# Three embedding blocks computed ahead of the first projection, and three filler units fewer in the attention of a one-core hybrid encoder step

## The chip, the cores and the metric

The kernel runs on one core of a Trainium2 chip. The metric is the device time of one execution in microseconds. The profile is one execution, taken by the hardware profiler; its times are counted from the start of its span. The engines are PE (TensorE: matrix products; PEld is its loading of weights), DVE (VectorE), ACT (ScalarE), POOL (GpSimd) and SP, which here only issues DMAs.

## The reference

One layer of a streaming encoder, on 1056 frames (1024 of a prompt and 32 of a sample) of width 1024:

- RMSNorm, then one projection whose columns are queries, keys and values of 8 heads, three parts of a gated convolution, and two sets of sigmoid gates ("gates", 2 x 1024 columns);
- stick-breaking attention (no softmax: products of 1 - beta over the keys between), and a causal convolution of width 3;
- both branches projected, weighed by their gates, summed, projected, added to x;
- RMSNorm, an MLP with squared ReLU (4096 wide), added to x;
- `x = x + sigmoid(rmsnorm(x) @ w_ple_gate) * (p @ w_ple)`, where p (1056 x 256) is an input of its own; then a final RMSNorm.

The change is about `p @ w_ple`. It depends on inputs alone, and the kernel calls its eight column blocks of 128 the embeddings. They are needed only in the last stage.

## The kernel before, in words

Everything is kept transposed: 128 features on the partitions, frames along the free axis. A float32 product is made of three products of rounded parts: each operand is split into a high part (ACT casts it, `fp32r`) and a low part (DVE subtracts the high part), and high x high, high x low and low x high are summed in PSUM.

The stages are: the first gates (lines 590 to 628), the rest of the input projection by a seven-product scheme (`seven`, line 209), the attention (lines 1062 to 1091), the branches and the output projection, the MLP (`up` and `down`), and the last stage with the embeddings. Inside a stage that stands under `tc.manual_schedule` the order on PE, ACT, DVE and POOL is the order in which the code issues the work. SP's order, and the branches, are placed by the framework's scheduler.

**The start.** SP issues, in this order, the weights of the first gate block, the first quarter of x in four pieces (`load_x`, line 285), the weights of the second block, and the other x. `vecT` goes through ACT's queue. In `first_gates` a round makes one group of 24 products, 264 columns wide. `prepare_plain` (line 162) casts and splits a block of weights (lines 98 and 99), `parts_x` (line 323) makes the high (line 329) and low (`mix`, line 142) parts of x, for eight pieces in the order 0, 2, 4, 6, 1, 3, 5, 7. The group's products are lines 203, 204 and 205; line 597 copies a finished group from PSUM. A pool `wraw` holds four blocks of raw weights, `wsp` two of split ones, `bpool` 34 buffers of one row block each. Six PSUM buffers take the groups in turn (`group`).

**The attention.** It has 64 steps: 4 pairs of heads, 2 heads each, 8 blocks of queries (step index i from 0 to 7, with i + 1 key blocks). The steps are software-pipelined by hand. In each round of the loop, in the order "LSAFBFG": L runs DVE's scan of the step before (line 799), S the scores of this step (PE lines 781 and 782, ACT sigmoid line 785, POOL mask line 792), A and B turn the weights of two steps before (PE line 835, ACT line 838, DVE line 839), G multiplies with the values (PE line 854) and F fills.

**Filler units.** F gives PE work that is free of the attention: gate blocks 10 to 15 (four units each, a unit being 24 products of 264 columns) and the eight embeddings (`embed_unit`, one unit each: 3 column tiles of 352, six products each, lines 735 to 737, an ACT copy of each tile, line 738, and one write to DRAM). They go in that order. Six units run before the attention (`START`), the other 26 (`FILL`) in it. `last_gates`, which holds gate blocks 14 and 15, also loads p and `w_ple` (`p_fetch`) and, after one of its groups each, splits the two halves of p (`p_parts`) and the two halves of `w_ple` (`embed_weights`). These four splits therefore come after 15, 16, 17 and 18 units of the attention's fill.

`pace` (line 1033) shares the units over the steps. It works out a load for every step from the sizes of three neighbouring steps, by and large DVE's work, and PE's own work; a step's part of FILL is what PE's own work leaves open of a fixed multiple of its load. Four times it adds 1.25 of load where the fill passes `FILL - 11 + more`:

```python
for more in (0, 1, 2, 3, None):
    unit = (FILL * 2.92 + sum(own)) / sum(load)
    part = [max(0.0, unit * v - o) for v, o in zip(load, own)]
    part = [x * FILL / sum(part) for x in part]
    ends = [sum(part[: n + 1]) for n in range(ns + 2)]
    if more is not None:
        load[next(n for n, e in enumerate(ends) if e > FILL - 11 + more)] += 1.25
```

## Time and profile before

| | us |
|---|---|
| median of 3 runs | 1553.07 |
| lowest and highest run | 1552.27, 1553.09 |
| the profiled execution's own time | 1552.95 |
| its span, first to last instruction | 1551.3 |
| PE, DVE, ACT busy | 1523.2, 1065.5, 745.2 |

The span is what the profile shows; the time holds 1.65 us more around it. A line of the profile names the engine, the line of the kernel, the operation, and what it writes and reads (`out<-in`, buffer numbers left out) with partitions x elements. "Idle before" is the engine's idle time just before the instruction, and the arrow names what ended it. PE's products overlap: each lasts longer than the time from its start to that of the next, so the pace is read from the start times. The first product starts at 6.17 us; the attention's scans run from 394.4 to 578.9.

### The profile page before, as it was taken

What the parts mean: (1) busy time and instruction counts of PE and PEld (TensorE: products, weight loads), DVE (VectorE), ACT (ScalarE), POOL (GpSimd) and SP (SyncE); (2) the same over time, 40 slices, a digit from 0 to 9 for tenths busy, and PEclk for the clock granted to TensorE, in tenths of its full rate; (3) what the DMA queues carried; (4) which work ended last, traced back from release to release, by engine and by line L of the source; (5) the groups of instructions that cost most, each with busy time, mean ns of one, the idle gap of its engine ahead of it and who ended that gap; (6) DMA issues with size and microseconds to landing.
All of it is one profiled execution on the core that took longest, in us unless ns stands there. A gap on an engine that the chain in (4) does not pass through costs nothing.

```text
span 1551.3 us, 29314 instructions
## 1 busy us (share of the span) xinstructions
PE 1523.2 (98%) x11770; PEld 1507.9 (97%) x11770; DVE 1065.5 (69%) x1414; ACT 745.2 (48%) x1357; POOL 347.3 (22%) x296
## 2 busy tenths in 40 slices
PE   8999999999999999999999999999999999999996
PEld 7999999999899999999999999999999999999996
DVE  7544776666778886766667555554577987799766
ACT  6643344443566774333355555555533334434544
POOL 1222332220211114001312222221020222013353
PEclk9999999999999999999999999999999999999998
DMA  6532155544635566335454344434886897583433
GB/s 230 199 113 78 34 184 201 191 151 115 210 100 153 167 222 231 98 129 180 162 187 147 138 142 149 153 132 144 295 305 201 264 343 250 191 269 109 134 116 118
DMA packets 111159, 268.97 MB, mean 173 GB/s; under 512 B 13456, under 2 KB 29328, under 8 KB 111024
## 3 DMA queue, kind: packets, MB, share of 16 engines
q1 hardware_dynamic: 110880, 267.08, 51.0%
q8 instruction: 92, 1.51, 0.4%
q14 instruction: 43, 0.35, 0.1%
q10 hardware_dynamic: 144, 0.03, 0.0%
HBM read 186.33 MB, written 80.73 MB: 172 GB/s over the span
## 4 chain that ended last, share of the span: by engine, by line
PE 86%; DVE 6%; ACT 2%; issue 2%; POOL 2%; DMA 2%; SPq 0%; DVEq 0%; POOLq 0%; ACTq 0%
PE ps_dn L1449 7%; PE ps_dn L1448 7%; PE ps_dn L1450 7%; PE ps_A11u L204 4%; PE ps_A11u L205 4%; PE ps_A11u L203 4%; PE ps_A11i L205 3%; PE ps_A11i L203 3%; PE ps_A11i L204 3%; PE av L854 2%; PE ps_wo L107 2%; PE ps_wo L108 2%; PE ps_wo L109 2%; PE ps_S1u L204 2%; PE ps_S1u L205 2%
## 5 line engine op out<-in xcount | busy, mean ns | idle before, releaser
L1449 PE MATMUL ps_dn<-fl,whi_dn 128*128 128x264 f32 x896 | 254.8, 284 | 0.1
L1450 PE MATMUL ps_dn<-fh,wlo_dn 128*128 128x264 f32 x896 | 254.8, 284 | 0.0
L1448 PE MATMUL ps_dn<-fh,whi_dn 128*128 128x264 f32 x896 | 254.8, 284 | 0.0
L1449 PEld LDWEIGHTS ps_dn<-fl,whi_dn 128*128 128x128 f32 x896 | 168.6, 188 | 0.4 <-DVE fl L1357 0.4
L1450 PEld LDWEIGHTS ps_dn<-fh,wlo_dn 128*128 128x128 f32 x896 | 168.7, 188 | 0.0
L1448 PEld LDWEIGHTS ps_dn<-fh,whi_dn 128*128 128x128 f32 x896 | 168.6, 188 | 0.0
L190 POOL TENSOR_TENSOR s_i<-raw_i,raw_i 128x512 f32<-128x512 f32 x30 | 40.8, 1359 | 228.9 <-DVE slS_i L153 196.0
L1341 DVE TENSOR_TENSOR wlo_dn<-raw_dn,whi_dn 128x1024 fp32r<-128x1024 f32 x40 | 71.0, 1776 | 25.5 <-ACT whi_dn L1335 24.9
L799 DVE TENSOR_TENSOR_SCAN r<-r 128x128 f32<-128x128 f32 (+3 forms) x64 | 86.6, 1353 | 2.2 <-POOL r L792 2.1
L1335 ACT CAST whi_dn<-raw_dn 128x1024 fp32r<-128x1024 f32 x40 | 42.0, 1051 | 93.3 <-PE ps_dn L1449 79.1
L190 POOL TENSOR_TENSOR s_u<-raw_u,raw_u 128x512 f32<-128x512 f32 x30 | 44.6, 1488 | 186.7 <-DVE slS_u L153 157.8
L1390 POOL TENSOR_TENSOR c<-c,rs 128x528 f32<-128x528 f32 x16 | 26.8, 1673 | 244.4 <-DVE c L1457 122.7
L1357 DVE TENSOR_TENSOR fl<-mr,fh 128x1056 fp32r<-128x1056 f32 x56 | 69.7, 1246 | 4.4 <-ACT fh L1352 4.4
L792 POOL TENSOR_SCALAR_AFFINE_SELECT r<-r 128x128 f32<-128x128 f32 x64 | 26.0, 407 | 204.5 <-ACT r L785 204.4
L153 DVE TENSOR_TENSOR slS_i<-s_i,shS_i 128x512 fp32r<-128x512 f32 x45 | 35.3, 788 | 51.7 <-ACT shS_i L151 51.5
L203 PE MATMUL ps_A11u<-T,shS_u 128*128 128x264 f32 x240 | 68.5, 285 | 0.0
L203 PE MATMUL ps_A11i<-T,shS_i 128*128 128x264 f32 x240 | 68.5, 285 | 0.0
L205 PE MATMUL ps_A11i<-T,slS_i 128*128 128x264 f32 x240 | 68.4, 285 | 0.0
L204 PE MATMUL ps_A11u<-T,shS_u 128*128 128x264 f32 x240 | 68.2, 284 | 0.0
L204 PE MATMUL ps_A11i<-T,shS_i 128*128 128x264 f32 x240 | 68.2, 284 | 0.0
L205 PE MATMUL ps_A11u<-T,slS_u 128*128 128x264 f32 x240 | 68.2, 284 | 0.0
L839 DVE TENSOR_TENSOR at<-pa,at 128x512 fp32r<-128x512 f32 (+2 forms) x96 | 50.9, 550 | 19.7 <-ACT at L838 19.3
(428 smaller groups left out, 5594.5 us busy)
## 6 DMA issues: line engine op xcount, KB each, us to landing
raw_dn<-in_w_down_dram SPq DMA_DIRECT2D x56, 512.0 KB, 4.5
raw_i<-in_w_in_dram SPq DMA_DIRECT2D x34, 512.0 KB, 4.6
mr<-mdT SPq DMA_DIRECT2D x32, 528.0 KB, 5.3
raw_u<-in_w_up_dram SPq DMA_DIRECT2D x32, 512.0 KB, 3.5
mdB<-m SPq DMA_DIRECT2D x48, 264.0 KB, 2.4
mr<-mdB SPq DMA_DIRECT2D x24, 528.0 KB, 6.3
raw_pg<-in_w_ple_gate_dram SPq DMA_DIRECT2D x17, 512.0 KB, 3.5
s<-gd SPq DMA_DIRECT2D x16, 528.0 KB, 5.6
```

What stands on the lines that cost most here:

```text
L190: f()
L203: nc.tensor.matmul(p_, wh[:, k, :], o[:, 0, c], start=new and n == 0, stop=False, **on)
L204: nc.tensor.matmul(p_, wh[:, k, :], o[:, 1, c], start=False, stop=False, **on)
L205: nc.tensor.matmul(p_, wl[:, k, :], o[:, 0, c], start=False, stop=z, **on)
L799: nc.vector.tensor_tensor_scan(rev, rev, rev, 1.0, ALU.mult, ALU.bypass)
L839: nc.vector.tensor_tensor(al, pt[:, :nb, :], ah.bitcast(F32), op=ALU.subtract)
L1335: nc.scalar.copy(hi, dws[u])
L1341: dve(lo, raw, hi.bitcast(F32), op=sub)
L1357: dve(l, mraw.pop(v), opd[v].bitcast(F32), op=sub)
L1448: nc.tensor.matmul(ps, hi[:, j, :], oh, start=j == 0, stop=False)
L1449: nc.tensor.matmul(ps, hi[:, j, :], ol, start=False, stop=False)
L1450: nc.tensor.matmul(ps, lo[:, j, :], oh, start=False, stop=j == NP_ - 1)
```

## The change

Ahead of all other loads SP now fetches the first three blocks of `w_ple` and p, p in three column tiles of each half. `first_embeds`, called before the first gates, multiplies a tile of ones with itself seven times (`WARM`), splits weights and p, and computes embeddings 0, 1 and 2 for all three column tiles: 9 groups of 6 products. Of the nine copies from PSUM the first three stand at its end on ACT, the middle three on DVE between the two halves of the first `parts_x`, the last three on ACT ahead of the second `parts_x`. The filler keeps embeddings 3 to 7, so `FILL` is 23. The later load of `w_ple` takes the five blocks that are left, two in the first half and three in the second; p is loaded a second time as before.

```diff
-FILL = 26.0
+FILL = 23.0
+FIRST_EMBEDS = 3
+WARM = 7
...
+    NE = FIRST_EMBEDS
+    pw_first = wraw.tile([P, NE, 2, P], F32, tag="raw", name="raw_pw_first")
+    nc.sync.dma_start(pw_first, w_ple[:, :NE])
+    p_first = [blk(f"pf{f}") for f in range(2)]
+    for c in ts:
+        for f in range(2):
+            nc.sync.dma_start(p_first[f][:, c], pT[f][:, c])
     n_ = base["g"]
     raws["i0"] = [raw_w(w_in, n_, KD, "i0_0")]
...
+    def first_embeds():
+
+        wu = gps.tile([P, TW], F32, tag="g", name="warm")
+        for _ in range(WARM):
+            nc.tensor.matmul(wu[:, :P], ones, ones, start=True, stop=True)
+        wh = wsp.tile([P, NE, 2, P], F32R, tag="whi", name="whi_pw_first")
+        wl = wsp.tile([P, NE, 2, P], F32R, tag="wlo", name="wlo_pw_first")
+        h, l = ([blk(f"pf{x}{f}", F32R) for f in range(2)] for x in "hl")
+        e = [blk(f"em{n}") for n in range(NE)]
+        late = []
+
+        def out():
+            n, c, ps = late.pop(0)
+            (nc.vector.tensor_copy if c is ts[1] else nc.scalar.copy)(e[n][:, c], ps)
+            if c is ts[-1]:
+                nc.sync.dma_start(ed[n], e[n])
+
+        nc.scalar.copy(wh, pw_first)
+        for i, c in enumerate(ts):
+            for f in range(2):
+                r = p_first[f][:, c]
+                nc.scalar.copy(h[f][:, c], r)
+                if i + f == 0:
+                    dve(wl, pw_first, wh.bitcast(F32), op=sub)
+                dve(l[f][:, c], r, h[f][:, c].bitcast(F32), op=sub)
+            for n in range(NE):
+                ps = group(f"ps_pw{n}_{i}")
+                for k in range(2):
+                    nc.tensor.matmul(ps, wh[:, n, k, :], h[k][:, c], start=k == 0, stop=False)
+                for k in range(2):
+                    nc.tensor.matmul(ps, wl[:, n, k, :], h[k][:, c], start=False, stop=False)
+                for k in range(2):
+                    nc.tensor.matmul(ps, wh[:, n, k, :], l[k][:, c], start=False, stop=k == 1)
+                late.append((n, c, ps))
+        for _ in range(NE):
+            out()
+        return out
...
-                parts_x(0, near_)
+                parts_x(0, near_, (0, 2, 4, 6))
+                for _ in range(NE):
+                    embed_out()
+                parts_x(0, near_, (1, 3, 5, 7))
                 prepare_plain("i0", 1)
             elif n in (1, 3):
+                if n == 1:
+                    for _ in range(NE):
+                        embed_out()
                 parts_x(n // 2, far_ if n == 1 else whole_)
...
-            pwr.append(wraw.tile([P, 4, 2, P], F32, tag="raw", name=f"raw_pw{i}"))
-            nc.sync.dma_start(pwr[i], w_ple[:, 4 * i : 4 * i + 4])
+            pwr.append(wraw.tile([P, 3, 2, P], F32, tag="raw", name=f"raw_pw{i}"))
+            nc.sync.dma_start(pwr[i][:, 1 - i :], w_ple[:, 3 + 2 * i : 5 + 3 * i])
...
-    units += [embed_unit(n) for n in range(KD)]
+    units += [embed_unit(n) for n in range(NE, KD)]
...
         nc.scalar.preload_act_table_set("sqrt_and_others")
+        embed_out = first_embeds()
         run(first_gates())
```

More of the change, by code (lines that the diff above doesn't have):

```diff
@@ L718, in embed_weights @@
     def embed_weights(i):
-        h, l = (blk(f"pw{i}{x}", F32R, [P, 4, 2, P]) for x in "hl")
-        nc.scalar.copy(h, pwr[i])
-        dve(l, pwr[i], h.bitcast(F32), op=sub)
+        h, l = (blk(f"pw{i}{x}", F32R, [P, 3, 2, P])[:, 1 - i :] for x in "hl")
+        nc.scalar.copy(h, pwr[i][:, 1 - i :])
+        dve(l, pwr[i][:, 1 - i :], h.bitcast(F32), op=sub)
         pw.append((h, l))
@@ L729, in body @@
                 conv_parts(n - 3)
-            wh, wl = (x[:, n % 4] for x in pw[n // 4])
+            wh, wl = (x[:, n - (3 if n < 5 else 5)] for x in pw[n >= 5])
             e = blk(f"em{n}")
```

## The prediction

> **What bounds the kernel now.** I read the page first: its busy rows and the chain of waits by engine.

> ```profile
> span 1551.3 us, 29314 instructions
> PE 1523.2 (98%) x11770; PEld 1507.9 (97%) x11770; DVE 1065.5 (69%) x1414; ACT 745.2 (48%) x1357; POOL 347.3 (22%) x296
> PE 86%; DVE 6%; ACT 2%; issue 2%; POOL 2%; DMA 2%; SPq 0%; DVEq 0%; POOLq 0%; ACTq 0%
> ```

> TensorE is busy 98% of the span and carries 86% of the chain. The change takes no product away: it moves 54 from the attention to the start and adds seven idle ones. So it can win only where PE now stands still or runs slowly, and can lose only where another engine gets too little PE work beside it. Two stretches decide: the first 13 us and the attention (about 394 to 586). First the timeline of the start (start, duration, engine, line):

> ```profile
> 0.80 0.39 SPq L89 DMA_DIRECT2D raw_i<-in_w_in_dram  x1
> 0.90 0.17 DVE L76 MEMSET ones<- 128x128 f32 x1 [0.90 <-PEq L1823]
> 1.25 1.96 SPq L287 DMA_DIRECT2D x<-in_xf_dram  x4
> 4.66 1.04 ACT L98 CAST whi_i<-raw_i 128x1024 fp32r<-128x1024 f32 x1 [2.14 <-DMA raw_i<-in_w_in_dram]
> 6.17 0.59 PE L203 MATMUL ps_g<-B,whi_i 128*128 128x264 f32 x1 [6.17 <-ACT B L329]
> 7.71 2.14 ACT L329 ACTIVATE B<-x,vecT 128x264 fp32r<-128x264 f32 x5 [0.22 <-DMA x<-in_xf_dram]
> 8.02 0.42 PE L203 MATMUL ps_g<-B,whi_i 128*128 128x264 f32 x1
> 10.00 0.42 PE L203 MATMUL ps_g<-B,whi_i 128*128 128x264 f32 x1
> 10.53 0.30 PE L203 MATMUL ps_g<-B,whi_i 128*128 128x264 f32 x1
> 11.76 0.28 PE L204 MATMUL ps_g<-B,whi_i 128*128 128x264 f32 x1
> 12.09 0.39 PE L205 MATMUL ps_g<-B,wlo_i 128*128 128x264 f32 x1
> ```

> PE does nothing for 6.17 us. From 8.02 to 10.00 nine products start 0.22 us apart; from 10.53 to 11.76 ten start 0.123 apart. So the first 4 us of work run at about half pace. The product at 12.09 is the 27th (third of the second gate group) and the last that waits early. At full pace 26 products take 3.2 us, so the gate stream stands as if it had begun at 8.9.

> The windows view shows the full clock even there, so half pace is read from start times, not from that column (PE, PEld, DVE, ACT, POOL, clock, DMA share, GB/s):

> ```profile
> 0.00:10.00 10.00, 3.17 (x12) 2.87 (x13) 4.36 (x11) 6.07 (x11) 0.70 (x6) 1.00 0.82 281
> 10.00:15.00 5.00, 4.95 (x39) 4.73 (x39) 4.56 (x10) 4.41 (x10) 0.00 (x0) 1.00 1.06 389
> 448.50:469.10 20.60, 20.60 (x165) 20.06 (x164) 19.13 (x27) 14.34 (x34) 3.17 (x8) 1.00 0.44 133
> 469.10:489.00 19.90, 19.90 (x159) 19.34 (x158) 18.07 (x26) 12.89 (x31) 2.90 (x8) 1.00 0.58 164
> 514.50:537.50 23.00, 22.70 (x161) 21.26 (x160) 21.00 (x29) 17.26 (x40) 5.10 (x8) 1.00 0.62 194
> ```

> The last three are rounds of eight attention steps. PE is full, but DVE works 19.13 of 20.60 us: PE bounds, with DVE 7 to 9% behind. Who makes PE wait in the attention (total, times, longest):

> ```profile
> PE z L781 <- ACT r L785: 1.0, 2, 0.5
> PE pa L835 <- DVE r L799: 1.0, 2, 0.8
> ```

> **The change part by part.** *Taken from the attention.* Two products five apart within one embedding group, and the group's ACT copy:

> ```profile
> 581.23 0.33 PE L736 MATMUL ps_pw<-p0l,pw1h 128*128 128x352 f32 x1
> 582.04 0.60 PE L835 MATMUL pa<-ident,r 128*128 128x128 f32 x4
> L738 ACT COPY em<-ps_pw 128x352 f32<-128x352 f32 x24 | 11.0, 457 | 4.9 <-PE ps_pw L737 4.5
> ```

> Five products in 0.81 us, 0.1625 each. Three units are 54 products: 54 x 0.1625 = **8.8 us** less PE work, and nine copies (4.1 us) less on ACT.

> *The start.* Seven DMAs (384 KB of weights, six of 176 KB; 1.47 MB) go ahead of everything in SP's queue. At 389 GB/s everything behind them lands 3.8 us later. I time the path from the rows above and these, of the groups of the first 40 us:

> ```profile
> L146 ACT CAST T<-x 128x528 fp32r<-128x528 f32 x7 | 4.1, 632 | 0.0
> L147 DVE TENSOR_TENSOR T<-x,T 128x528 fp32r<-128x528 f32 x7 | 4.5, 691 | 0.0
> L99 DVE TENSOR_TENSOR wlo_i<-raw_i,whi_i 128x1024 fp32r<-128x1024 f32 x4 | 4.9, 1217 | 5.1 <-ACT whi_i L98 5.1
> L597 ACT COPY sg<-ps_g 128x264 f32<-128x264 f32 x9 | 3.4, 374 | 3.7 <-PE ps_g L205 3.6
> ```

> The first weights land at 4.66 less 128 KB (0.34 us): 4.3; the pieces of p follow 0.46 apart, 4.8 to 7.1. ACT: high part of the weights (three quarters of 1.04) to 5.1, then six pieces. No 352-wide cast from SBUF is in the trace; it lies between 0.374 (264 wide) and 0.632 (528); I take 0.40, nearest the first: done at 5.5, 5.9, ... 7.5. DVE: low weights (three quarters of 1.217) to 6.0, then low pieces, bounded by half and whole of 0.691; I take 0.5: 6.5, 7.0, ... 9.0. The first group's sixth product needs the second low piece: it ends at about 7.15. Nothing is late for the other 48: 48 x 0.1625 = 7.8, so the embeddings end at **14.95** at full pace.

> Is the gate work ready then? Gate weights land at 4.66 + 3.8 = 8.5; ACT is first done with the three early copies (9.55), casts to 10.6, and makes eight high parts at 0.43 (2.14 / 5) by 14.05. Their last x lands at 7.7 + 3.8 = 11.5, read at 11.9. DVE follows to 11.8, four low parts to 13.5, three copies to 14.9, four low parts to 16.5. The first of those is needed by the 14th gate product, 14.95 + 13 x 0.123 = 16.55, and is ready at 15.3. The second gate weights wait for the buffer that the last embedding product frees: cast to 16.0, low part behind DVE's queue to 17.75, needed at 18.15. So no wait, if only by 0.4 us. The later x are used one, two gate groups on, with the same distance as now. The three writes of finished embeddings stand in SP's queue between the weights of the next set and wait for the last copies (17.4); behind them waits

> ```profile
> POOL s_i L190 <- DMA raw_i<-in_w_in_dram: 22.5, 1, 22.5
> ```

> POOL, whose sums before began at 22.6 and are first multiplied after 16 gate groups (8.9 + 16 x 2.95 = 56): 30 us of room, so no cost.

> The 27th gate product then starts at 14.95 + 3.2 = 18.15 instead of 12.09: **+6.1 us**, for 8.8 us of work done.

> *The clock.* The ones are set at 1.07, so seven products run from about 1.1. What they last, from the same kind (ones against a full-float tile: nine products in 18 instructions, first and last start given):

> ```profile
> L391 PE MATMUL pr<-dg,ones x18: 195/275/377, 83.6 to 85.6; 128*128 128x128 f32 x16, 128*128 128x32 f32 x2
> ```

> 2.0 us over 17 steps is 0.118 per instruction; seven products are 14, at half pace 0.21 each: 3.0 us, until 4.1. Then 1.4 us idle until 5.5. Before, about 4 us of work ended half pace. Price of no effect: from 7.15 to 9.6 products at 0.29 instead of 0.1625, some 6.6 lost: 1.1 us. I count full pace.

> [...]

> *What the attention gives back.* Its planner shares FILL over the steps by DVE load. Working through pace(): a round gets 2.25 to 2.34 units instead of 2.68, 1.0 to 1.2 us less PE work. DVE's free time there is 1.5 (20.60 - 19.13) and 1.8 us: covered. Two places are not.

> First, entry. To 406.98 the chain is not PE's:

> ```profile
> 397.44 3.98 DMA q<-qd
> 405.37 1.56 DVE r L799
> 406.98 0.66 PE pa L835 x4
> ```

> Units left out of steps 0 to 4 (1.99 to 1.82, 0.5 us) only lengthen that wait.

> Second, the planner adds 1.25 of load at four fill positions from FILL - 11 on, where p and its weights are split. Those splits hang in gate units, which stay at positions 15 to 18; the four bumps now stand at 12 to 15. Before, bumps fell on steps 37, 39, 40, 44 and splits on 39, 40, 40, 44. Now bumps fall on 32, 35, 38, 40 and splits on about 40, 43, 47, 49.

> ```profile
> L115 DVE TENSOR_TENSOR p0l<-pr,p0h 128x1056 fp32r<-128x1056 f32 x1 | 1.3, 1259 | 0.2 <-ACT p0h L114 0.2
> L721 DVE TENSOR_TENSOR pw0l<-raw_pw,pw0h 128x1024 fp32r<-128x1024 f32 x1 | 1.2, 1225 | 0.3 <-ACT pw0h L720 0.3
> L99 DVE TENSOR_TENSOR wlo_oc<-raw_oc,whi_oc 128x512 fp32r<-128x512 f32 x2 | 1.4, 684 | 0.0
> ```

> Each bump is 0.44 unit, 1.3 us of PE work; three are misplaced: 3.9 us without cover. DVE's free time over those ten steps, 1.9 us, takes up half. I count 2.0 us of new PE waits (bounds: minus the 1.0 us that PE now waits for ACT, if fewer copies end that; plus 3.9).

> **Sum:** +6.1 - 8.8 + 0.5 + 2.0 = -0.2 us on the profiled execution's 1552.95. The median of the runs is 1553.07, 0.1 higher; I predict 1552.8.

> **Rivals.** (a) *The attention pays in full*: DVE's slack hides the misplaced bumps and the ACT waits go: +6.1 - 9.8, and -0.6 if loads and splits come a little earlier: -4, 1549. For it: PE waits little on DVE before, with rounds at 91 to 93%. Against: round 514.5 has DVE at 21.00 of 23.00 and already 0.3 us of PE gap, with its bumps in place. (b) *The attention becomes DVE's*: around steps 40 to 50 every uncovered microsecond turns into a PE wait (3.9 and the entry 0.5, plus 1 where ACT's p casts hold up a sigmoid): +6.1 - 8.8 + 5.4 = +2.7, with the cold clock +3.8: 1556.7. It turns slower once the new waits exceed 2.7 us. (c) *The ones do not hold the clock*: +1.1, 1553.9 with the rest as forecast; that part then doesn't do what it says.

> **Numbers.** A measurement of this kernel tells about 0.2%, 3.1 us, from no change. Forecast, with (c) on its own inside the same band: 0.64. (a) beyond -3.1: 0.20. (b) beyond +3.1: 0.16. The range reaches into (a) and (b): 1549.4 to 1556.2.

> **What would show it.** Third product of the second gate group at 18.1; earlier is better. Embedding products at 0.16 from the first (0.29: (c)). Attention from first to last scan shorter by about 6 us; new "PE pa <- DVE r" waits of about 2 us near steps 43 to 50, their absence means (a), over 4 us (b). Behind the attention nothing should move. The forecast is wrong if gate weights, not PE, end the start, or if the early loads of the next weights hold up POOL's sums.

## The result, and the profile after

| | before | changed | ratio, 95% interval |
|---|---|---|---|
| first comparison, median (lowest to highest, runs) | 1552.89 (1552.27 to 1553.84, 6) | 1558.79 (1556.17 to 1560.41, 6) | 1.0034 [1.0022, 1.0045] |
| on another chip (e1) | 1553.04 (1551.55 to 1556.34, 19) | 1556.95 (1555.47 to 1557.99, 11) | 1.0021 [1.0012, 1.0030] |
| profiled execution, span | 1551.3 | 1558.1 | |

The change makes the kernel slower, by 3.9 to 5.9 us. The forecast was 1552.8 with a range up to 1556.2. The changed kernel's page, answering to the three lines shown first of before:

```profile
span 1558.1 us, 29376 instructions
PE 1527.9 (98%) x11784; PEld 1510.7 (97%) x11784; DVE 1073.9 (69%) x1424; ACT 746.2 (48%) x1361; POOL 353.8 (23%) x296
PE 86%; DVE 5%; issue 3%; ACT 2%; POOL 2%; DMA 1%; SPq 0%; POOLq 0%; DVEq 0%; ACTq 0%
```

The page alone says nothing: 4.7 us more PE time, and nearly the same shares. The places are told by comparing start times of the same instructions (us later than before; first run: the profiled execution above; e1: the same kernel again; e9: a variant below):

| | before at | changed | e1 | e9 |
|---|---|---|---|---|
| 27th gate product | 12.09 | +8.3 | +9.1 | +9.2 |
| first seven-product group | 56.64 | +9.2 | +8.8 | +8.8 |
| first scan of the attention | 394.40 | +8.4 | +7.5 | +7.8 |
| first conv-branch product | 582.60 | +4.2 | +3.2 | +3.5 |
| first attention-branch product | 631.81 | +8.0 | +5.1 | +3.5 |
| end of span | 1551.30 | +6.8 | +4.0 | +2.3 |

So the start costs 8 to 9 us, the attention gives 4.3 back, and the branch stage behind it, in which nothing was to move, takes 2 to 4 us in two of the three. The start of the changed kernel (timeline; a row may join equal instructions, "x2"):

```profile
0.80 0.39 SPq L296 DMA_DIRECT2D raw_pw_first<-in_w_ple_dram  x1
5.27 0.33 SPq L91 DMA_DIRECT2D raw_i<-in_w_in_dram  x1
5.11 0.83 ACT L349 CAST whi_pw_first<-raw_pw_first 128x768 fp32r<-128x768 f32 x1 [2.58 <-DMA raw_pw_first<-in_w_ple_dram]
5.84 2.56 ACT L353 CAST pfh<-pf 128x352 fp32r<-128x352 f32 x6
12.07 1.05 ACT L100 CAST whi_i<-raw_i 128x1024 fp32r<-128x1024 f32 x1
1.12 3.33 PE L336 MATMUL warm<-ones 128*128 128x128 f32 x14 [1.12 <-DVE eps_t L80]
6.38 0.82 PE L360 MATMUL ps_pw<-pfh,whi_pw_first 128*128 128x352 f32 x2 [1.93 <-ACT pfh L353]
8.90 0.79 PE L362 MATMUL ps_pw<-pfh,wlo_pw_first 128*128 128x352 f32 x2
17.27 0.28 PE L205 MATMUL ps_g<-B,whi_i 128*128 128x264 f32 x1
20.41 0.28 PE L207 MATMUL ps_g<-B,wlo_i 128*128 128x264 f32 x1
```

The first weights are cast at 5.11 instead of 4.3, the first embedding product runs at 6.38 instead of 5.5 (PE's first useful product before ran at 6.17: the embeddings start no earlier than the gates did), from 8.31 to 10.66 pairs of products stand 0.59 apart (0.29 each), and the gates begin at 17.27. There was no wait between the embeddings and the gates, as forecast, and the 27th product follows 3.14 later (3.2 forecast). In this one profile the clock column tells more (windows, columns as in the prediction):

```profile
4.30:7.71 3.41, 1.49 (x6) 0.86 (x5) 1.74 (x3) 2.60 (x6) 0.00 (x0) 1.00 1.01 354
7.71:11.12 3.41, 3.40 (x12) 3.27 (x12) 1.83 (x5) 1.60 (x4) 0.00 (x0) 0.50 0.97 319
```

The column's first entry in this trace is at 4.30, at the end of the ones (1.12 to 4.45), and it is 1.00; PE was busy for only 1.49 of the 3.41 us from there, and the next 3.41 us ran at 0.50.

Rounds of eight scans in the attention (windows, columns as before; 1st and 2nd answer to the first two rounds shown of before, the 3rd to the third), and the branch stage:

```profile
454.85:475.49 20.64, 20.36 (x159) 19.28 (x158) 19.11 (x27) 14.12 (x32) 4.54 (x8) 1.00 0.53 141
475.49:497.13 21.64, 20.61 (x161) 19.47 (x160) 19.16 (x26) 13.80 (x32) 4.42 (x8) 1.00 0.52 159
521.82:544.57 22.75, 21.87 (x170) 20.54 (x169) 20.45 (x29) 16.29 (x39) 4.63 (x8) 1.00 0.40 124
```
```profile
610.00:614.00 4.00, 3.45 (x20) 2.87 (x18) 3.45 (x2) 2.58 (x3) 3.72 (x2) 1.00 0.94 373
614.00:618.00 4.00, 2.75 (x9) 2.76 (x10) 4.00 (x3) 1.08 (x1) 3.35 (x2) 0.66 0.24 74
```
```profile
614.00:618.00 4.00, 4.00 (x26) 3.95 (x26) 3.20 (x6) 2.35 (x3) 0.00 (x0) 1.00 0.63 235
```

The last fence is the kernel before. The first round did not get shorter (20.60 before); it is a weak witness, because it holds nearly the same filler work (60 filler products against 61), but PE now has gaps, of 0.3 to 1.0 us in each of the three. In the branch stage PE has 9 products in 4 us where before had 26, with the clock column at 0.66. What PE waited for in the attention (engine, line, total us, times, longest):

```profile
PE pa L888 <- DVE r L852: 2.2, 4, 0.8
PE z L834 <- ACT r L838: 1.7, 4, 0.5
PE pas L1069 <- DMA raw_pw<-in_w_ple_dram: 1.5, 1, 1.5
```

Before, the first two were 1.0 and 1.0, and the third was not there. Its row names a DMA that `pas` does not read; in e1 the same wait is put down to DVE's `oT` (line 812), and in the timeline of this profile `oT` ends at 424.60, behind a scan of 2.02 us, and the product starts at 424.65. It too is a wait for DVE. The branch stage's timeline shows what PE waits for:

```profile
611.51 3.13 POOL L941 TENSOR_TENSOR s<-s,rs 128x1056 f32<-128x1056 f32 x1 [0.28 <-DMA raw_oc<-in_w_conv_out_dram]
612.89 2.30 DVE L101 TENSOR_TENSOR wlo_oc<-raw_oc,whi_oc 128x512 fp32r<-128x512 f32 x1 [0.55 <-ACT whi_oc L100]
615.25 0.66 PE L111 MATMUL ps_oc<-cv,wlo_oc 128*128 128x352 f32 x1 [1.75 <-DVE wlo_oc L101]
615.70 0.49 PE L109 MATMUL ps_oc<-cv,whi_oc 128*128 128x352 f32 x1
```

DVE's low part of the weights takes 2.30 us beside a POOL multiplication (0.68 to 0.69 in the three of this stage that have none beside them); PE waits 1.75 us and then runs its products 0.29 apart instead of 0.16. So there are four questions: the start, the attention, the branch stage, and why the same kernel spreads from 1555.5 to 1560.4.

### The profile page after: what moved, and what is told of

Same layout as the page of the kernel before. It is cut to its first block, busy times and chain, and to the rows that moved or that the text cites. A ratio compares the mean times of both kernels' runs of the same rounds, so it can differ in the third digit from the quotient of the medians.

```text
span 1558.1 us, 29376 instructions
## 1 busy us (share of the span) xinstructions
PE 1527.9 (98%) x11784; PEld 1510.7 (97%) x11784; DVE 1073.9 (69%) x1424; ACT 746.2 (48%) x1361; POOL 353.8 (23%) x296
## 4 chain that ended last, share of the span: by engine, by line
PE 86%; DVE 5%; issue 3%; ACT 2%; POOL 2%; DMA 1%; SPq 0%; POOLq 0%; DVEq 0%; ACTq 0%
PE ps_dn L1504 7%; PE ps_dn L1503 7%; PE ps_dn L1502 7%; PE ps_A11u L206 4%; PE ps_A11u L207 4%; PE ps_A11u L205 4%; PE ps_A11i L207 3%; PE ps_A11i L205 3%; PE ps_A11i L206 3%; PE av L907 2%; PE ps_wo L109 2%; PE ps_wo L111 2%; PE ps_wo L110 2%; PE ps_S1u L206 2%; PE ps_S1u L205 2%
## 5 line engine op out<-in xcount | busy, mean ns | idle before, releaser
L845 POOL TENSOR_SCALAR_AFFINE_SELECT r<-r 128x128 f32<-128x128 f32 x64 | 32.8, 514 | 194.6 <-ACT r L838 194.5
L205 PE MATMUL ps_A11i<-T,shS_i 128*128 128x264 f32 x240 | 68.6, 286 | 0.0
L205 PE MATMUL ps_A11u<-T,shS_u 128*128 128x264 f32 x240 | 68.6, 286 | 0.0
L1406 ACT CAST fh<-mr 128x1056 fp32r<-128x1056 f32 x56 | 60.1, 1073 | 6.2 <-DMA mr<-mdB 6.2
```

What stands on the lines that cost most here:

```text
L205: nc.tensor.matmul(p_, wh[:, k, :], o[:, 0, c], start=new and n == 0, stop=False, **on)
L1406: nc.scalar.copy(h, mraw[v])
```

## The experiments

My theory after the result: the start costs what its loads and a half-pace clock cost; the attention gives back only half, since DVE and ACT bound it as soon as PE has less to do; and waits of about 2 us, followed by half pace, come on top. Rivals stand with each run. All ratios are to the kernel before on the same chip.

### The halves

**e1_again**: the changed kernel, no edit.

> The changed kernel once more, unedited. Its runs so far spread over 4.2 us (1556.2 to 1560.4), those of before over 1.6. Theory 'clock windows': two half-clock windows of 3.4 us (one at the start, one in the branch stage at 615 us) come and go between executions; a second profile then shows at least one of them gone, or moved, and the time changes by about 1.7 us for each. Theory 'fixed schedule': both windows and the PE waits stand where they stood, 1558 to 1560.

1556.95, ratio 1.0021 [1.0012, 1.0030]. The start and the attention are as in the first profile (table above); the branch stage takes 1.9 us instead of 3.8: PE still waits 1.4 us for low weights, but no half pace follows, and at the start half pace lasts to 12.7 us. The stretches come and go, as the first theory has it.

**e2_head_alone**: early embeddings, and all eight once more in the attention.

```diff
-FILL = 23.0
+FILL = 26.0
...
-    units += [embed_unit(n) for n in range(NE, KD)]
+    units += [embed_unit(n) for n in range(KD)]
```

(Left out: the later load and split of `w_ple` take all eight blocks again.)

> Only the start is changed: embeddings 0 to 2 are computed first, but the attention keeps all 26 filler units and computes them a second time. Theory 'the start is dear': the third product of the second gate group at about 20.4 (it was at 12.1), and nothing behind makes up for it: 1552.9 + 8 to 9 = 1561 to 1562. Theory of the prediction: +6.1, 1559.0, and the rest of the loss of the changed kernel is in the attention or behind it.

1562.40 (5 runs), ratio 1.0053 [1.0039, 1.0067]. The 27th gate product is 8.9 us late, the first conv product still 8.9: with the attention's work put back, it returns nothing. The branch stage then adds 3.7.

**e3_attention_alone**: the start of the kernel before, embeddings 0 to 2 left out and gate values written in their place.

```diff
-FILL = 26.0
+FILL = 23.0
+NE = 3
...
+                if 2 * s_ + i < NE:
+                    nc.sync.dma_start(ed[2 * s_ + i], r)
...
-    units += [embed_unit(n) for n in range(KD)]
+    units += [embed_unit(n) for n in range(NE, KD)]
```

> Only the attention is changed: 23 filler units, the start as before. Embeddings 0 to 2 are not computed; gate values are written in their place, so part of the last stage's result is left out of the computation. Theory of the prediction: 8.8 us less PE work, 2.5 given back: 1546.6. Theory 'the branches take it': the attention ends 4 to 6 us earlier, but the branch stage behind it is held by its gate values (DMA, POOL, DVE) and gives up to 4 back: 1548 to 1552, with a PE wait for wlo_oc of over 1 us.

1550.26 (9 runs), ratio 0.9979 [0.9969, 0.9988]. Work worth 8.8 us was left out, and 2.8 us came back; in its profile the attention, first scan to first conv product, is 3.9 us shorter. This is the size that the whole change rests on, free of the start.

**e4_bumps_back**: the four bumps of load three units later, where the splits are.

```diff
-                load[next(n for n, e in enumerate(ends) if e > FILL - 11 + more)] += 1.25
+                load[next(n for n, e in enumerate(ends) if e > FILL - 8 + more)] += 1.25
```

> The changed kernel with the planner's four extra loads at fill positions 15 to 18 (FILL - 8), where the splits of p and of its weights are issued. Theory 'misplaced cover': 2 us of PE waits for DVE go from the steps 40 to 50, about 1.5 us off the time at an unchanged start. Theory 'the attention is bound by DVE anyhow': the waits move and the time stays within 0.5 us of the changed kernel's.

1559.77 (1556.24 to 1561.08, 5 runs), ratio 1.0033 [1.0020, 1.0046]: no faster. Yet in its profile the attention is 5.8 us shorter than before's instead of 4.3. Where that is lost again is taken up under "The sum".

**e14_attention_bumps**: e3 with the same edit.

> e3_attention_alone (start of the kernel before, embeddings 0 to 2 left out and gate values written in their place, FILL 23) with the four bumps of load moved back by three units, to where the splits are (FILL - 8 + more). It gives the attention's part alone, without the start. e3 was 3.0 us shorter than the kernel before for 8.8 us of PE work less. Theory 'misplaced bumps take 1.5 us, the rest of the shortfall are waits for DVE and ACT in all rounds': 4.3 to 5.0 us shorter (ratio 0.9968 to 0.9972). Rival 'the bumps are the shortfall' (the prediction counted 2.0 to 3.9 us for them): 6.5 to 8 us shorter (ratio 0.995 to 0.9958).

1549.50 (11 runs), ratio 0.9978 [0.9969, 0.9987]; the attention is 5.2 us shorter, 1.3 more than e3's. In the profiles the misplaced bumps are 1.3 to 1.6 us of the attention, by e3 against e14 and the changed kernel against e4; at the medians the move brings nothing (2.8 us below the kernel before with it and without it), and in the pair e9 and e18 below the attention gets 0.5 us longer by it. What is left of the shortfall stands in its waits:

```profile
PE pa L838 <- DVE r L802: 1.8, 3, 0.8
PE pas L1018 <- DMA raw_pw<-in_w_ple_dram: 1.4, 1, 1.4
PE z L784 <- ACT r L788: 1.3, 3, 0.5
```

With the bumps in place PE still waits 4.5 us for these three, where before it waited 2.0 for the first and the third.

**e8_six_out**, **e12_six_out_conv**: e3 with six embeddings left out.

```diff
-FILL = 26.0
+FILL = 20.0
+NE = 6
...
-                load[next(n for n, e in enumerate(ends) if e > FILL - 11 + more)] += 1.25
+                load[next(n for n, e in enumerate(ends) if e > FILL - 5 + more)] += 1.25
```

e12 alone has this as well, since the embeddings also start the reading of the conv branch's parts:

```diff
-            if 3 <= n < 7:
-                conv_parts(n - 3)
+            if n == 6:
+                for i in range(4):
+                    conv_parts(i)
```

> As e3_attention_alone (the start of the kernel before, fewer filler units), but six units fewer in place of three: FILL is 20, the embeddings 0 to 5 are not computed and gate values are written in their place, so the last stage adds other numbers; p and all its weights are loaded and split as before, and the four bumps of load stand where the splits are. 17.5 us of PE work leave the attention. e3 gave 3.0 us for 8.8. Theory 'the attention is bound by DVE's chain as soon as PE has less work': the second three units bring at most 3 us, so 3 to 6 us in all (ratio 0.996 to 0.998), with PE waiting for DVE and ACT for over 8 us more than before. Rival 'only the misplaced bumps cost': each unit brings nearly its 2.9 us, 13 to 17 us in all (ratio 0.989 to 0.9915).

1542.17, ratio 0.9929 [0.9917, 0.9942], but this time says nothing of the attention: the embeddings that were dropped also held the reading of three of four conv blocks, and three quarters of the conv branch's products were gone.

> e8_six_out once more, with the conv parts read back as before: in e8 the embeddings that were left out had also held the reading of three of the four conv blocks, so that three quarters of the conv branch's products were missing and its branch stage says nothing. Here only the embeddings 0 to 5 are left out (17.5 us of PE work) and gate values written in their place. e8's attention, first scan to first conv product, was 4.8 us shorter. Theory 'the attention gives back little more than e3's 3 us since PE then waits for DVE and ACT, and a long wait halves the clock': attention 4 to 8 us shorter than before's 188.2 us, ratio 0.9945 to 0.998. Rival 'only the place of the bumps costs': 13 to 17 us shorter, ratio 0.989 to 0.9915.

1549.46 (1546.31 to 1550.55, 6 runs), ratio 0.9971 [0.9960, 0.9983]. In the profile, that of the fastest run, the attention is 7.6 us shorter than before's, for 17.5 us of work: the second three embeddings bring 2.4 us more than e14's three, of 8.7. At the medians they bring 1.1.

```profile
PE pa L840 <- DVE r L804: 3.7, 7, 0.8
PE ps_pw L740 <- ACT pw1h L724: 1.9, 1, 1.9
PE zs L1002 <- DVE kk L998: 1.3, 1, 1.3
```

The waits for DVE's scans grow from 1.0 (before) over 1.8 (e14) to 3.7 us. The rival that only the bumps' place costs has fallen: it asked for 13 to 17 us. Two things differ besides the work left out: e12 reads all four conv parts at one place, and its first embedding product waits 1.9 us for weights that are split too late.

### The start

**e5_warm0**: no products of ones. **e6_warm16**: sixteen instead of seven.

```diff
-WARM = 7
+WARM = 16
```

(This is e6's edit; e5 takes out the tile and the loop.)

> The changed kernel without the products of ones. In three of the four profiles that have the early embeddings (e1_again, e2_head_alone, e4_bumps_back) the embedding products begin at half pace all the same, and the third product of the second gate group starts at 20.9 to 21.2 us. Theory 'seven ones bring nothing': it starts at 20.9 to 21.2 here too, and the time is that of the changed kernel (1557 to 1559, ratio to the kernel before 1.002 to 1.0035). Rival, the step on record (the ones lift the clock): without them 1.1 us later, 22.0 to 22.3, and 1.1 us slower (ratio 1.003 to 1.0045).

1557.22 (6 runs), ratio 1.0028 [1.0016, 1.0041]. The 27th gate product starts at 19.83: not 1.1 us later without the ones, but 0.6 to 1.4 earlier. Two-microsecond windows of e1 (seven ones) and e5 (none); the second bracket's count is of PE's products:

```profile
8.50:10.50 2.00, 2.00 (x9) 2.00 (x7) 1.09 (x3) 0.51 (x2) 0.00 (x0) 1.00 0.97 326
10.50:12.50 2.00, 2.00 (x8) 2.00 (x8) 0.00 (x0) 0.69 (x2) 0.00 (x0) 1.00 1.07 387
```
```profile
8.50:10.50 2.00, 2.00 (x11) 2.00 (x10) 1.10 (x3) 0.82 (x3) 0.00 (x0) 1.00 1.03 343
10.50:12.50 2.00, 2.00 (x14) 2.00 (x13) 0.00 (x0) 1.48 (x4) 0.00 (x0) 1.00 1.04 393
```

Without ones PE is at full pace (14 products) from 10.5 on; with them it is still at half (8). The clock column stands at 1.00 in all four rows, so the pace must be read from the counts. In the six profiles with seven ones the 27th gate product starts at 20.41 to 21.26, in the three without (e5, e15, e17) at 19.83 to 20.39. That the ones delay it is not shown. Full clock comes at 12.72 in e1 and at 9.58 in e5. In e1 PE is busy for 84% of the 3.41 us from 5.89 to 9.30, and half pace goes on for 3.41 us more; in e5 it is busy for 92% of the 3.41 us ahead of 9.58, and full pace follows. Why is not shown. Without ones or early embeddings full clock comes at 10.3 to 10.8 in four profiles, but at 13.0 and 13.8 in two (e12, e14). What is shown is that seven ones bring nothing that lasts: the step on record is wrong.

> The changed kernel with sixteen products of ones (32 instructions) in place of seven. They last until about 7 us at half pace, past the arrival of the first weights, so PE never stands idle between 1.1 us and the embeddings. Theory 'what failed is the idle time between the ones and the first embedding product (4.45 to 6.38 us)': the embedding products run 0.16 apart from the first, the third product of the second gate group starts near 19 instead of 20.9 to 21.2 us, and the time falls by 1.5 to 2 us (ratio 1.001 to 1.002). Rival 'what failed is the weights and parts that land later than forecast': it starts at 20.4 or later, with PE waiting for casts, and the time is that of the changed kernel.

1559.46 (5 runs), ratio 1.0036 [1.0023, 1.0048]. Sixteen do lift the clock: the windows from 8.5 to 12.5 count 15 and 14 products where e5 has 11 and 14. But the 27th gate product starts at 19.55, only 0.3 earlier than without any, because PE is at the products of ones until the first embedding product at 7.65, 1.3 later than in the changed kernel; and the time is no better. I had expected 19.

**e11_loads_only**: the kernel before with the seven early loads, which nothing reads.

```diff
+    pw_first = wraw.tile([P, 3, 2, P], F32, tag="raw", name="raw_pw_first")
+    nc.sync.dma_start(pw_first, w_ple[:, :3])
+    p_first = [blk(f"pf{f}") for f in range(2)]
+    for c in ts:
+        for f in range(2):
+            nc.sync.dma_start(p_first[f][:, c], pT[f][:, c])
```

> The kernel before with the seven early loads (1.47 MB of weights and p) ahead of all others, and no early embeddings: nothing reads what they bring. It tells the loads' part of the late start from the products' part. Theory 'the loads alone push the gates back by what they take at 389 GB/s': the third product of the second gate group starts at 15.5 to 16.0 instead of 12.09 us (3.4 to 3.9 later), the whole is 3 to 4 us longer (ratio 1.002 to 1.0026), so the products add the other 4.6 to 5.3 us of the 8.3 to 9.1 measured. Rival 'the loads fit beside the first casts': under 1.5 us later, ratio under 1.001, and the products cost all of it.

1558.87 (1556.85 to 1560.19, 7 runs), ratio 1.0034 [1.0023, 1.0045]: the loads alone cost as much as the whole change. The 27th gate product is 5.75 us late.

```profile
5.33 0.33 SPq L89 DMA_DIRECT2D raw_i<-in_w_in_dram  x1
10.01 1.04 ACT L98 CAST whi_i<-raw_i 128x1024 fp32r<-128x1024 f32 x1 [7.50 <-DMA raw_i<-in_w_in_dram]
11.58 0.59 PE L203 MATMUL ps_g<-B,whi_i 128*128 128x264 f32 x1 [11.58 <-ACT B L335]
```

The gate weights are cast 5.35 us later, not 3.8. The DMA view of the first 16 us in 40 slices of 0.4 us shows why, before and e11:

```profile
GB/s 0 0 0 0 92 0 102 435 376 370 366 386 388 375 372 357 380 387 443 369 364 378 359 364 362 364 354 375 380 396 396 391 401 412 380 412 396 407 386 396
DMA packets 3560, 5.15 MB, mean 322 GB/s; under 512 B 352, under 2 KB 2400, under 8 KB 3560
```
```profile
GB/s 0 0 0 0 100 150 128 189 204 238 317 333 373 391 394 401 365 312 309 369 337 337 297 279 298 301 325 320 373 358 442 396 414 370 377 380 380 383 383 375
DMA packets 3549, 4.68 MB, mean 292 GB/s; under 512 B 406, under 2 KB 3141, under 8 KB 3549
```

Before, the rate is up at 2.8 us; with the early loads it climbs to that only at about 5 us, and sags again between 6.4 and 11 us. By 16 us 4.68 MB have moved instead of 5.15; the missing 0.47 MB take 1.2 us at 389 GB/s, which would be most of the excess of 1.55.

**e13_loads_three**: as e11, p in two whole halves.

```diff
-    for c in ts:
-        for f in range(2):
-            nc.sync.dma_start(p_first[f][:, c], pT[f][:, c])
+    for f in range(2):
+        nc.sync.dma_start(p_first[f], pT[f])
```

> As e11_loads_only, with p in two whole halves of 528 KB instead of six strips of 176 KB: three early DMAs instead of seven, the same bytes, again read by nothing. In e11 the gate weights are cast at 10.01 instead of 4.66 us (5.35 later where the bytes at 389 GB/s make 3.8), their DMA is issued only at 5.33, and the DMA engines, though busy, move 100 to 240 GB/s in their first 3 us. Theory 'the strips and the late issue cost the excess': cast at 8.4 to 9.0, third product of the second gate group at 15.9 to 16.6 instead of 17.84, 1.3 to 1.8 us less than e11. Rival 'it is the bytes at the rate of the start, however they are cut': 17.4 to 18.2, time as e11.

1556.90 (8 runs), ratio 1.0028 [1.0017, 1.0038]. Cast at 9.49, 27th gate product at 17.34: 0.5 us less than e11 and 1.0 us more than the bytes make at 389 GB/s, so the rival is nearer. The strips and the issues that go with them are 0.5 us of the excess; that the rest is the slow rate alone fits, and no run shows it.

**e7_before_ones**: the kernel before with fourteen products of ones ahead of its gates.

```diff
+        wu = gps.tile([P, TW], F32, tag="g", name="warm")
+        for _ in range(14):
+            nc.tensor.matmul(wu[:, :P], ones, ones, start=True, stop=True)
```

> The kernel before with fourteen products of ones (28 instructions, from about 1.1 to 7 us) ahead of its first gates, and nothing else. In the kernel before the first products are 0.22 us apart and full pace comes only at about 10.4 us. Theory 'an unbroken run of idle products lifts the clock': the gate products are 0.123 apart from their first, the third product of the second gate group starts at 10.8 to 11.2 instead of 12.09 us, and the whole is 0.9 to 1.3 us shorter (ratio 0.9991 to 0.9994). Rival 'the first products are bound by the casts of x and the weights, not by the clock': no difference, or up to 0.6 us longer since the ones end behind the arrival of the first weights.

1558.12 (1556.71 to 1560.22, 5 runs), ratio 1.0034 [1.0022, 1.0047], the surprise of the study. The ones lift the clock (16 products in the window 8.5 to 10.5 where before has 11) and the gates gain nothing: the 27th starts at 12.03 instead of 12.09, so the clock did not bound this stretch: PE now stands still between products (1.25 of 2.00 us busy from 10.5 to 12.5), waiting for the parts. Yet the end is 5.2 us later. In its profile 2.0 us come at one place, where the kernel before has the same wait:

```profile
203.00:206.00 3.00, 1.01 (x8) 0.81 (x8) 1.75 (x3) 2.29 (x5) 0.93 (x1) 1.00 0.79 322
206.00:210.00 4.00, 4.00 (x22) 4.00 (x21) 4.00 (x4) 0.90 (x2) 3.23 (x3) 0.57 0.36 139
```
```profile
203.00:206.00 3.00, 1.50 (x12) 1.29 (x11) 2.26 (x3) 1.79 (x5) 1.35 (x2) 1.00 0.71 289
206.00:210.00 4.00, 4.00 (x35) 4.00 (x34) 4.00 (x4) 1.66 (x4) 3.31 (x2) 1.00 0.35 139
```

The first fence is e7, the second before. PE idles 2.0 instead of 1.5 us of the three, and then e7 alone runs four microseconds at a clock of 0.57, 13 products short. Another 3.2 us come in the branch stage, where two products start 1.68 us apart and a stretch of half clock follows in the same way. PE waits there for ACT's high part of the weights, not for DVE's low part (so too in e2, 1.7 us): ACT does it behind a gate activation, which waits for DVE multiplications of 3.1 and 3.5 us beside POOL's, where one without POOL beside it takes 1.25.

### The branch stage

**e9_after_dve**: the changed kernel, gate multiplications of the conv branch on DVE. **e10_before_dve**: the kernel before with the same edit. **e16_before_ones_dve**: e7 with it.

```diff
-                sgs["c"] = gate_values(8 + n, pool)
+                sgs["c"] = gate_values(8 + n, dve)
```

> The changed kernel with the conv branch's eight gate multiplications (s<-s,rs of 1056 columns) on DVE instead of POOL. In the profile of the changed kernel DVE's low part of the conv weights lasts 2.30 us beside a POOL multiplication and 0.68 without one; PE waits 2.07 us for it, and the next 3.4 us run at half the clock (profiles of the changed kernel, e2 and e6), which costs 3.7 us together. Theory 'the two time levels of the changed kernel (1556 to 1557 and 1559 to 1560.5) come from this wait': without POOL no product waits 1 us or more in this stage, no half-pace stretch follows, the stage from the first conv product to the first attention product takes 49.2 to 49.6 us, all runs stand together, and the median falls to 1555 to 1556 (ratio to the kernel before 1.0013 to 1.002). Rival 'DVE is then the bound of the stage' (it is busy 42 of 56 us in the kernel before, and gets 8 x 1.25 us more): longer waits than 2 us, same time or slower.

1555.76 (1554.71 to 1557.67, 11 runs), ratio 1.0015 [1.0006, 1.0024]. No wait of PE is left in the stage, the table's +3.5 stays +3.5, and no half pace follows:

```profile
610.00:614.00 4.00, 4.00 (x27) 4.00 (x26) 4.00 (x7) 1.87 (x3) 0.00 (x0) 1.00 0.93 366
614.00:618.00 4.00, 4.00 (x26) 4.00 (x26) 3.16 (x4) 2.95 (x4) 0.00 (x0) 1.00 0.80 244
```

The times alone do not tell it from e1 (1.0021 [1.0012, 1.0030], with POOL in place and no run above 1558); that this wait makes the upper level of the changed kernel's times rests on the profiles.

> The kernel before with the same single edit (the conv branch's gate multiplications on DVE instead of POOL). Its profile has two short waits for low weights in this stage, 0.27 and 0.43 us. Theory: they go and nothing else changes, 0 to 0.8 us shorter (ratio 0.9995 to 1.0), and its rarer slow executions (up to 1556) go too. Rival 'DVE is the bound of the stage': 1 to 5 us longer. If it is no slower it is the kernel to beat, and the changed kernel's loss is then measured without the branch stage's lottery.

1552.27 (11 runs), ratio 0.9992 [0.9983, 1.0001]: 1.1 us better at the median, a little more than expected, but not told apart from no change. No kernel of the study that computes everything is faster.

> e7_before_ones (the kernel before with fourteen products of ones ahead) with the conv branch's gate multiplications on DVE. e7 did not move the first gates (12.03 against 12.09 us), and yet was 5.2 us longer: 2.0 after a wait of 2.26 us at 203 us with 3.4 us at half the clock behind it, 3.2 in the branch stage with another such stretch behind a wait of 1.68 us. Theory 'the ones change nothing but when the clock's windows begin, and the windows decide whether a wait of about 2 us is followed by half pace': the branch stage's 3.2 us go with its wait, and the stretch at 206 us may stay (up to 2 us): 1552.3 to 1554.5, and the profile shows no half pace behind 590 us. Rival 'the ones cost in some other way': 1556 or more.

1554.29 (11 runs), ratio 1.0009 [1.0000, 1.0017]. The branch stage's 3.2 us are gone (it is 0.4 shorter than before's), and the span is 2.5 longer; in its profile half pace follows the wait at 203 us again, and 1.7 us more come at 400 to 408 us, where another such stretch follows a wait of 1.76 us for `kk`. Why the ones still cost 2.0 us at the median is not shown.

### The sum

**e15_mended**, **e17_mended_again**: no ones, bumps back, multiplications on DVE. **e18_ones_dve_bumps**: e9 with the bumps back.

> The changed kernel with three of its losses taken away at once: no products of ones, bumps moved back by three units, the conv branch's gate multiplications on DVE. If the accounts of e4, e5 and e9 add up: the median of e9 (1555.76, 2.3 to 2.9 above the kernel before) less 1.5 for the bumps, less 0 to 1 for the ones: 1553.3 to 1554.3 (ratio 1.0 to 1.0006), no run above 1556. What is left is then the price of the start itself (8 us later) against an attention 5.8 us shorter. Rival 'something else in the changed kernel costs': 1555 or more.

> e15_mended unedited (the changed kernel without ones, bumps moved back, gate multiplications on DVE), once more. Its runs lay at 1555.5 to 1559.7 where 1553.3 to 1554.3 was expected; its profile (the fastest run, 1555.5) holds a branch stage without waits and an attention 5.7 us shorter than the kernel before, and a seven-product stage of the MLP that is 1.4 us longer than elsewhere (411 instead of 413 products in 50 us, with no waits). Theory 'chance of that sample': 1553.5 to 1556 here. Rival 'without ones the start is slower in most runs': again 1557 or more, and if the profile falls on such a run it shows where (third product of the second gate group behind 21 us, or half pace behind a wait).

> The changed kernel with its seven ones, the gate multiplications on DVE and the bumps moved back by three units: e9_after_dve and one more edit. e9 was 1555.76, all eleven runs at 1554.7 to 1557.7. Theory 'the bumps' place is worth 1.5 us whatever else is in the kernel': 1553.8 to 1554.8 (ratio 1.0003 to 1.0012). Rival 'moving the bumps gains in the attention's records and is lost again elsewhere (e4 was no faster than the changed kernel)': 1555.5 or more.

1557.94 (5 runs, 1.0034 [1.0021, 1.0046]), 1556.60 (11 runs, 1.0022 [1.0013, 1.0031]) and 1557.18 (11 runs, 1.0021 [1.0012, 1.0030]): all three missed, and none is faster than e9. Against before, their attention is shorter by 5.7 (e15) and 4.8 us (e17), more than e9's 4.3, but by 3.8 in e18, where PE waits 2.0 us for the load of q. But the MLP's first stage, in which nothing was changed, takes 310.06 us from its first seven-product group to the first product of `down`, in all four kernels with early embeddings and the bumps back (e4, e15, e17, e18), and 308.62 in the changed kernel, e1, e5 and e9. (In the other kernels it takes 308.0 to 308.9.) Two hundred microseconds of it, e9 and e17:

```profile
850.00:1050.00 200.00, 200.00 (x1645) 200.00 (x1644) 105.64 (x159) 108.03 (x207) 53.66 (x39) 1.00 0.41 144
```
```profile
850.00:1050.00 200.00, 200.00 (x1636) 200.00 (x1635) 105.64 (x158) 107.06 (x205) 53.57 (x39) 1.00 0.41 144
```

PE has no gap in either, and still starts 9 products fewer. Over the whole stage that is 1.44 us, about what the bumps had gained. What makes the difference is not shown.

## Why the prediction was wrong

- **"They end at 14.95 at full pace ... the 27th gate product then starts at 18.15: +6.1"**: wrong by 2.3 to 3.1 us. The embeddings start 0.9 later than forecast, because the first weights land 0.8 later; and 54 products take 10.9 us instead of 9.45, half pace lasting until about 11 (first profile). A 352-wide cast from SBUF is in the trace before, against what the prediction says (line 871, three times, 0.484 us on average); it mattered little, as the six casts took 0.43 each where 0.40 was counted. The start of the gates behind them without a wait was right.
- **"I count full pace"**: wrong. Seven ones end 1.9 us before the first embedding product and lift nothing that lasts: full pace begins at 12.1 to 12.7 us in five of the six profiles with them. In the sixth, the first one taken, the clock column reads 1.00 from 4.30, PE is busy for 1.49 of the next 3.41 us, and half pace follows from 7.71 to 11.12. In the changed kernel without ones it ends at 9.6 to 10.7 (three profiles). The rival (c), priced at +1.1, was the case, and "that part then doesn't do what it says" holds. That seven would do was the author's estimate: in the kernel before full pace came behind about 4 us of work, and the ones were to last 3.0.
- **"At 389 GB/s everything behind them lands 3.8 us later"**: 5.35 for the gate weights in e11. It did not end the wait here, because PE was still at the embeddings, but it says what the plan could be worth: even with embeddings for nothing the start would be 5.75 us late, for 8.8 us of work that the attention returns by half.
- **"Covered"**, the step that failed in the attention: 1.0 to 1.2 us less PE work in a round was held against 1.5 to 1.8 us of DVE's free time. From the first scan to the first conv product, before and changed:

```profile
394.40:582.60 188.20, 185.36 (x1414) 176.27 (x1412) 156.70 (x209) 123.71 (x289) 29.02 (x79) 1.00 0.55 169
402.84:586.77 183.93, 177.70 (x1359) 167.38 (x1357) 154.84 (x208) 118.72 (x279) 35.78 (x79) 1.00 0.53 162
```

PE's busy time falls by 7.7 of the 8.8 us, but its idle time grows from 2.84 to 6.23, and the stage gets only 4.3 shorter, while DVE is busy for 84% of it. It grows where PE waits for a scan, a sigmoid or `oT` (the rows above). Free time as a sum over a round does not say that a scan or a sigmoid is ready at the moment when PE comes earlier. The new wait of 1.5 us in the sample part (line 1069) was not seen at all; it stands between the third and the eleventh scan, where 12 filler products fewer (78 against 90) make the stretch only 0.15 us shorter (23.68 against 23.83). The next eight scans, also with 12 fewer, have no gap and take 2.0 us less: there the step held. Without start and bumps (e14) 5.2 of 8.8 came back where the sum allowed 8.3.
- **Entry 0.5, bumps 2.0**: the bumps measure 1.3 to 1.6 in the profiles of two pairs, inside the bounds, and -0.5 in a third; in the time no pair shows them. The entry was not tried by itself.
- **"Behind the attention nothing should move"**: wrong by 1.9 to 3.8 us. The order of the work did not move, its timing did, and a low part or a gate multiplication on DVE that happens to run beside a POOL multiplication comes late: in the changed kernel the low part takes 2.30 us instead of 0.69, the multiplication 3.07 instead of 1.25. e9 shows it by taking POOL out: the stage is as long as before.
- **Rival (b)**, slower by new DVE waits in the attention, had the sign and nearly the time (1556.7), but that was luck, for it had not the place: the attention lost 2.0 us against the forecast, the start 2.3 to 3.1.

The sum of e1, whose profiled 1557.01 is nearest to its median: start +8.8, won back before the attention -1.3, attention -4.3, branches +1.9, all behind them -1.1: +4.0 in the span. The -1.3 and the -1.1 were not traced to a cause.

**The spread.** The changed kernel's times spread over 4 us, e9's over 3. Waits of about 2 us are followed by some 3.4 us of half pace in some executions and not in others: behind 613 us in the changed kernel and e6 and not in e1, behind 203 us in e7 and e16 and not in before. The clock column shows a pattern. In the changed kernel it changes at 7.71, 11.12, 615.28, 618.69 and 1547.12 us, and between these lie 1, 177, 1 and 272 times 3.413 us; the two entries of before, 10.33 and 1539.50, lie 448 times 3.413 us apart. I call the stretches of 3.41 us that are counted from a change of the same trace its windows. Here are the window ahead of the half-pace stretch and the stretch itself, first in the changed kernel, then the two windows of the wait at 203 us in e10, which no half pace follows:

```profile
611.87:615.28 3.41, 1.62 (x10) 1.03 (x8) 2.86 (x3) 2.58 (x4) 3.25 (x2) 1.00 0.55 217
615.28:618.69 3.41, 3.41 (x12) 3.41 (x13) 3.41 (x3) 0.52 (x2) 2.23 (x1) 0.50 0.26 77
```
```profile
201.80:205.21 3.41, 1.61 (x13) 1.40 (x12) 1.08 (x3) 2.67 (x5) 0.25 (x1) 1.00 0.90 367
205.21:208.62 3.41, 3.40 (x28) 3.40 (x29) 3.41 (x2) 1.08 (x3) 3.21 (x2) 1.00 0.29 118
```

In the profiles of kernels that compute everything there are nine half-pace stretches between 100 and 1500 us; each is one window long and follows one in which PE was busy for 34 to 56%. An edge can divide a wait: the changed kernel's idle time from 212.06 to 213.77 us leaves its two windows 87 and 63% busy, and no half pace follows. Between 50 and 56% both outcomes occur. So PE did not stand idle for a whole window ahead of any of them: two products started 2.08 us apart in the changed kernel, 2.26 and 1.68 in e7. Why the window of e10, busy for 47%, is not followed by half pace and that of e16 (202.74 to 206.15), busy for 48%, is, stays open; e10's wait ends at 205.22, on the edge of its window.

## What to carry to other kernels

PE time taken out of a stage was a gain here only as far as the other engines' results were ready earlier too: try it by leaving the work out (e3 took one run and gave 2.8 of 8.8 us) before looking for another place for the work. An "empty" start was not free: the first product of data began at 6.17 us before and at 6.38 in the changed kernel, and the loads put in front made the cast of the gate weights 5.35 us later (e11), where their bytes at 389 GB/s make 3.8. A wait of 1.75 us, with the clock at 0.50 for 3.41 us behind it, cost the branch stage of the changed kernel 3.8.
